# Two heads side by side in TensorE's columns: values stationary, probabilities moving

## The chip, the cores and the metric

The kernel runs on one core of one Trainium2 chip. The metric is the device time of one execution in microseconds (us). The median of three runs of the kernel before is 3547.29 us (3547.2 to 3551.07).

## The reference

A two-layer encoder over 512 tokens of width 1024. Each layer has a mixing part with 8 retention heads and 8 dilated attention heads of width 64, a cross-attention to 256 memory rows, and a product-key expert layer. The change is in the mixing part:

```python
h = rms_norm(x, norm_mix[layer])
rq, rk, rv, rg, aq, ak, av = jnp.split(h @ w_in[layer], split_points, axis=-1)
ret = bidirectional_retention(rq, rk * HEAD_DIM ** -0.5, rv, log_gamma)       # 8 heads
ret_out = head_rms_norm(ret, ret_norm_gain[layer]) * jax.nn.silu(rg)
att = dilated_mixture_attention(aq, ak, av)                                   # 8 heads
att_out = head_rms_norm(att, att_norm_gain[layer])
x = x + jnp.concatenate([ret_out, att_out], axis=-1) @ w_out[layer]
```

With all 512 tokens in one block, retention of a head is (Q K^T, times a decay that depends on the distance of the two positions) V. The three dilated patterns of attention together are one softmax over 512 keys with an additive bias per head (the slope's distance term, and the logarithm of how many patterns see the key), times V. All values are float32.

## The kernel before

Tokens stand in 4 blocks of 128 (NB = 4). `mix` runs for each layer in these steps:

- The input is normed and transposed (`norm_rows`, `to_T`) into T_hi and T_lo, a split into two parts. Projections (`proj_T` at L174, `proj_N` at L190) multiply both parts with both parts of the weights, which SP's queue loads (`wload`) and ScalarE and VectorE split (`split`, L113 and L114).
- `heads` projects queries and keys for four heads at a time (u = 0, 1) and yields, head by head, q and two key operands.
- Retention: for each head VectorE and ScalarE make the decay tile dm (L338 to L340, two buffers). For each of 4 key blocks, s = K Q^T of all 512 queries (L345; s has two PSUM buffers), and VectorE multiplies s with a window of dm into pt (L348; five buffers). Then, for each query block and key block, a matmul with 128 columns of pt stationary and the head's 64 columns of values moving adds into po, a tile of 128 queries x 4 blocks x 64 (L353). ScalarE copies po to the head's columns of cat (L355).
- `N_out` (L190, with its copy at L325) then projects the gates and the attention's values, and `norm_heads` norms four heads at once.
- Attention: for each head the bias is loaded into a dm buffer (L370). For each query block: s = Q K^T (L375), bias and row maximum on VectorE (L379, L380), exp with the row's sum on ScalarE (L381), four transposes of p into PSUM tile t (L384, two buffers), a copy to pt (L387 on ScalarE or L389 on VectorE, by the query block), and four matmuls with pt stationary and 64 columns of values moving into po (L391). At the head's end VectorE divides po by the sums into cat (L393, L394). Before head 7 (KH = 7) the memory rows are normed (`mem_norm`). Every fourth head `norm_heads` runs.
- At the end the tiles of the early pool are released, the memory's keys are projected (`mem_kv`, L174), cat is transposed (L408) and multiplied with w_out (L190).

The po tiles alternate between PSUM banks named o and g. The order in which each engine gets its instructions is not the program's alone: a scheduler orders them with a timeline of its own (`TCK`), so that projections of later heads stand between the steps of a head. Behind `mix` follow the cross-attention and routing (`tail`) and the dense and sparse expert sums (L675, L715, L578 to L590), which the change leaves alone.

Of the kernel before, what the change touches and what calls it, by code (L numbers as in the profile page):

```python
# [8 lines left out]
F32 = mybir.dt.float32  # L9
# [6 lines left out]
AF = mybir.ActivationFunctionType  # L16
OP = mybir.AluOpType
# [5 lines left out]
S = 512  # L23
L = 2
NB = 4
# [5 lines left out]
HD = 64  # L31
EPS = 1e-6
WREL = 896
# [24 lines left out]
KH = 7  # L58
# [4 lines left out]
class Kernel:  # L63
# [225 lines left out]
    def norm_heads(self, sb, cat, gain, g, silu=None):  # L289
# [12 lines left out]
            nc.vector.tensor_mul(sq, sq, silu[:, :, c])  # L302
        nc.vector.tensor_mul(v, sq, gain[:, None, c].to_broadcast([128, NB, 256]))

    def mix(self, l, kvp):
        nc, a, ps = self.nc, self.a, self.ps
        with ExitStack() as st:
            early = ExitStack()
            ea = self.pool(early, "early")
            sb = self.pool(st, "late", side="right")  # L310
            gain = sb.tile([128, D], F32, name="gain")
            self.bcast_rows(gain, a["norm_mix"], l * D, D)
            hT = (sb.tile([128, KT, S], F32R, name="T_hi"), sb.tile([128, KT, S], F32R, name="T_lo"))
            if l == 0:
                self.load_x(1, 2, 3)
            for b, h in self.norm_rows(sb, self.x, gain, order=FIRST[l]):
                self.to_T(h, hT, b * 128)
            w = a["w_in"][l]

            def N_out(c0, silu=False, order=range(NB)):  # L320
                t = ea.tile([128, NB, 512], F32, name="rv", bufs=2)

                def evac(i, c, p):
                    o = t[:, i, c:c + 256]
                    nc.scalar.activation(o, p, AF.Silu if silu else AF.Copy)  # L325
                self.proj_N(w, c0, 512, hT, order, evac)
                return t

            rv = N_out(1024, order=FIRST[l])
            lg = self.log_gamma(sb, l)  # L330
            relp = ea.tile([128, WREL], F16, name="relp")
            nc.sync.dma_start(relp, a["relpos"])
            reln = ea.tile([128, WREL], F16, name="reln")
            nc.sync.dma_start(reln, a["relneg"])
            cat = sb.tile([128, NB, D], F32, name="cat")
            for h, q, ks in self.heads(ea, w, 0, 512, hT, 1.0, HD ** -0.5):
                dm = ea.tile([128, WREL], F32, name="dm", bufs=2)
                nc.vector.tensor_scalar(dm, relp, lg[:, h:h + 1], None, op0=OP.mult)  # L338
                nc.vector.scalar_tensor_tensor(dm, reln, lg[:, 8 + h:9 + h], dm, op0=OP.mult, op1=OP.add)
                nc.scalar.activation(dm, dm, AF.Exp)  # L340
                pts = []
                for kb in range(NB):
                    s = ps.tile([128, 512], F32, name="s", bufs=2)
                    for i in range(2):
                        nc.tensor.matmul(s, ks[i][:, kb * 128:(kb + 1) * 128], q, start=(i == 0), stop=(i == 1))  # L345
                    pt = ea.tile([128, 512], F32, name="pt", bufs=5)
                    o = 384 - 128 * kb
                    nc.vector.tensor_mul(pt, s, dm[:, o:o + 512])  # L348
                    pts.append(pt)
                po = ps.tile([128, NB, HD], F32, name="og"[h % 2])  # L350
                for qb in range(NB):
                    for kb in range(NB):
                        nc.tensor.matmul(po[:, qb, :], pts[kb][:, qb * 128:(qb + 1) * 128],  # L353
                                         rv[:, kb, h * HD:(h + 1) * HD], start=(kb == 0), stop=(kb == NB - 1))
                nc.scalar.activation(cat[:, :, h * HD:(h + 1) * HD], po, AF.Copy)  # L355

            gcat = sb.tile([128, D], F32, name="gain")
            self.bcast_rows(gcat[:, :512], a["ret_norm_gain"], l * 512, 512)
            self.bcast_rows(gcat[:, 512:], a["att_norm_gain"], l * 512, 512)
            silu = N_out(1536, True)  # L360
            for g in range(2):
                self.norm_heads(sb, cat, gcat, g, silu)
            av = N_out(3072)
            den = sb.tile([128, 8, NB], F32, name="den")
            rden = sb.tile([128, 8, NB], F32, name="rden")
            for h, q, ks in self.heads(ea, w, 2048, 2560, hT, HD ** -0.5, 1.0):
                if h == KH:
                    kT = self.mem_norm(l, sb)
                bias = ea.tile([128, WREL], F32, name="dm", bufs=2)
                nc.sync.dma_start(bias, a["att_bias"][h])  # L370
                po = ps.tile([128, NB, HD], F32, name="og"[h % 2])
                for qb in range(NB):
                    s = ps.tile([128, 512], F32, name="s", bufs=2)
                    for i in range(2):
                        nc.tensor.matmul(s, q[:, qb * 128:(qb + 1) * 128], ks[i], start=(i == 0), stop=(i == 1))  # L375
                    p = ea.tile([128, 512], F32, name="p", bufs=3)
                    m = ea.tile([128, 2], F32, name="m", bufs=4)
                    o = 384 - 128 * qb
                    nc.vector.tensor_tensor_reduce(p, s, bias[:, o:o + 512], 1.0, -3e38, OP.add, OP.max, m[:, 0:1])  # L379
                    nc.vector.tensor_scalar(m[:, 1:2], m[:, 0:1], -1.0, None, op0=OP.mult)  # L380
                    nc.scalar.activation(p, p, AF.Exp, bias=m[:, 1:2], accum_out=den[:, h, qb:qb + 1])  # L381
                    tp = ps.tile([128, 4, 128], F32, name="t", bufs=2)
                    for kb in range(NB):
                        nc.tensor.transpose(tp[:, kb, :], p[:, kb * 128:(kb + 1) * 128], self.ident)  # L384
                    pt = ea.tile([128, 4, 128], F32, name="pt", bufs=5)
                    if qb % 2:
                        nc.scalar.activation(pt, tp, AF.Copy)  # L387
                    else:
                        nc.vector.tensor_copy(pt, tp)  # L389
                    for kb in range(NB):  # L390
                        nc.tensor.matmul(po[:, qb, :], pt[:, kb, :], av[:, kb, h * HD:(h + 1) * HD],  # L391
                                         start=(kb == 0), stop=(kb == NB - 1))
                nc.vector.reciprocal(rden[:, h, :], den[:, h, :])  # L393
                nc.vector.tensor_mul(cat[:, :, 512 + h * HD:512 + (h + 1) * HD], po,  # L394
                                     rden[:, h, :, None].to_broadcast([128, NB, HD]))
                if h % 4 == 3:
                    self.norm_heads(sb, cat, gcat, 2 + h // 4)

            early.close()
            kv = self.mem_kv(l, self.pool(kvp, "kv"), kT)  # L400
            next(kv)
            cst = ExitStack()
            cp = self.pool(cst, "ct")
            cT = (cp.tile([128, KT, S], F32R, name="C_hi"), cp.tile([128, KT, S], F32R, name="C_lo"))
            for k in range(KT):
                pt = ps.tile([128, NB, 128], F32, name="t", bufs=2)
                for b in range(NB):
                    nc.tensor.transpose(pt[:, b, :], cat[:, b, k * 128:(k + 1) * 128], self.ident)  # L408
                self.split(cT[0][:, k, :], cT[1][:, k, :], pt.rearrange("p b t -> p (b t)"))
# [529 lines left out]
```

## Time and profile before

| | |
|---|---|
| median of 3 runs | 3547.29 us |
| profiled execution: its time, its span | 3550.38 us, 3548.6 us |
| TensorE matmuls busy (PE) | 3473.6 us, 98% |
| weight loads busy (PEld) | 3182.7 us, 90% |
| VectorE (DVE), ScalarE (ACT), GpSimd (POOL) | 75%, 41%, 20% |
| mean granted TensorE clock | 0.991 |

PE is TensorE's matmuls and PEld its weight loads, which overlap them; a matmul's record includes its way through the array, so records overlap as well, and a busy PE is not PE at its peak. The busy time of a record says less than the distance between the starts of two. A row of a group reads: line, engine, operation, written tile <- read tiles, shapes, count | busy time in us, mean ns of one | idle time before them and what ended it. A row of the order of time or of the chain reads: start in us, length in us, what, count. TensorE's operands are named moving first: `o<-rv,pt` has rv moving and pt stationary. A matmul of two full float32 operands shows as two records.

### The profile page before, as it was taken

How to read it: one execution, taken by the hardware profiler on the slowest of the kernel's cores; microseconds unless marked ns; L12 is line 12 of the kernel's file. 1: busy time of each engine (PE TensorE's matmuls, PEld its weight loads, DVE VectorE, ACT ScalarE, POOL GpSimd, SP SyncE). 2: the span in 40 equal slices, each digit the busy share in tenths (PEclk: the TensorE clock that was granted, in tenths of full speed). 3: DMA queues.
4: the chain of work that ended last, by engine and by line, in shares of the span. 5: the costliest groups of instructions: out<-in, count | busy, mean ns of one | idle time of the engine just before them, and what ended most of it. 6: DMA issues, size and time to landing. Idle time of an engine off the chain costs nothing.

```text
span 3548.6 us, 55359 instructions
## 1 busy us (share of the span) xinstructions
PE 3473.6 (98%) x20844; PEld 3182.7 (90%) x20844; DVE 2645.4 (75%) x5722; ACT 1470.2 (41%) x2210; POOL 699.7 (20%) x518
## 2 busy tenths in 40 slices
PE   8999999999999999999999999999999999999998
PEld 7989998999888888888889899989999888888887
DVE  5565559998677788888555655599995877888885
ACT  4453544455333333333333535445553333333332
POOL 0000000002334445444100000000022443444440
PEclk9999999999999999999999999999999999999999
DMA  5252444567989999999432424446689999999992
GB/s 163 74 144 84 146 136 138 207 224 285 389 302 350 341 340 332 340 340 337 154 98 79 133 90 155 133 135 218 220 300 378 328 337 343 344 332 341 343 335 94
DMA packets 428380, 848.42 MB, mean 239 GB/s; under 512 B 28112, under 2 KB 278992, under 8 KB 421968
## 3 DMA queue, kind: packets, MB, share of 16 engines
q1 hardware_dynamic: 321360, 488.32, 41.2%
q0 software_dynamic: 73728, 268.47, 20.8%
q10 hardware_dynamic: 33024, 88.10, 6.9%
q8 instruction: 163, 2.67, 0.3%
q14 instruction: 105, 0.86, 0.1%
HBM read 754.60 MB, written 77.59 MB: 235 GB/s over the span
## 4 chain that ended last, share of the span: by engine, by line
PE 90%; DVE 6%; DMA 2%; ACT 1%; issue 1%; SPq 0%; ACTq 0%; POOL 0%; DVEq 0%; POOLq 0%
PE pj L675 28%; PE pj L174 13%; PE s L715 10%; PE t L715 10%; PE pj L190 9%; PE o L715 5%; PE g L715 5%; PE s L345 1%; DVE w_lo L114 1%; PE g L391 1%; PE s L375 1%; PE t L384 1%; PE g L353 1%; PE o L353 1%; PE g L873 1%
## 5 line engine op out<-in xcount | busy, mean ns | idle before, releaser
L114 DVE TENSOR_TENSOR w_lo<-w_raw,w_hi 128x1024 fp32r<-128x1024 f32 x696 | 849.4, 1222 | 404.1 <-ACT w_hi L113 391.7
L113 ACT ACTIVATE w_hi<-w_raw 128x1024 fp32r<-128x1024 f32 x696 | 735.3, 1060 | 981.6 <-PE g L715 342.8
L578 POOL DMA_INDIRECT row<-in_expert_down,ei x256 | 339.0, 1324 | 2308.3 <-PE g L874 916.8
L675 PE MATMUL pj<-hT_hi,w_hi 128*128 128x384 f32 x2048 | 697.7, 341 | 12.8 <-ACT c L678 10.5
L675 PE MATMUL pj<-hT_lo,w_hi 128*128 128x384 f32 x2048 | 698.8, 341 | 0.0
L675 PE MATMUL pj<-hT_hi,w_lo 128*128 128x384 f32 x2048 | 696.0, 340 | 0.8 <-DVE w_lo L114 0.6
L578 POOL DMA_INDIRECT row<-in_expert_up,ei x256 | 360.0, 1406 | 454.2 <-DVE x L590 419.3
L675 PEld LDWEIGHTS pj<-hT_hi,w_hi 128*128 128x128 f32 x2048 | 386.3, 189 | 18.3 <-ACT c L678 11.1
L675 PEld LDWEIGHTS pj<-hT_hi,w_lo 128*128 128x128 f32 x2048 | 386.1, 189 | 5.6 <-DVE w_lo L114 2.4
L675 PEld LDWEIGHTS pj<-hT_lo,w_hi 128*128 128x128 f32 x2048 | 386.2, 189 | 4.4
L590 DVE SCALAR_TENSOR_TENSOR x<-row,act,x 128x1024 f32<-128x1024 f32 x256 | 327.7, 1280 | 6.0 <-DMA row<-in_expert_up,ei 4.6
L584 DVE SCALAR_TENSOR_TENSOR row<-row,hn 128x1024 f32<-128x1024 f32 x256 | 309.4, 1219 | 19.9 <-DMA row<-in_expert_down,ei 19.5
L113 ACT ACTIVATE ch<-c 128x384 fp32r<-128x384 f32 x128 | 67.0, 523 | 280.2 <-PE g L715 240.1
L715 PE MATMUL t<-w_lo,ch 128*128 128x512 f32 x512 | 160.7, 389 | 0.0
L715 PE MATMUL t<-w_hi,ch 128*128 128x512 f32 x512 | 159.6, 389 | 0.0
L715 PE MATMUL s<-w_hi,ch 128*128 128x512 f32 x512 | 158.5, 391 | 0.0
L715 PE MATMUL s<-w_lo,ch 128*128 128x512 f32 x512 | 158.1, 390 | 0.0
L190 PE MATMUL pj<-w_hi,T_hi 128*128 128x256 f32 x640 | 156.9, 286 | 0.9 <-ACT T_hi L113 0.5
L715 PE MATMUL s<-w_hi,cl 128*128 128x512 f32 x512 | 157.8, 389 | 0.0
L715 PE MATMUL t<-w_hi,cl 128*128 128x512 f32 x512 | 157.7, 389 | 0.0
L113 ACT ACTIVATE ch<-cd 128x384 fp32r<-128x384 f32 x128 | 66.6, 520 | 208.9 <-PE g L715 208.9
L174 PE MATMUL pj<-T_hi,w_hi 128*128 128x512 f32 (+1 forms) x512 | 150.0, 341 | 2.1 <-DVE qlo L260 1.8
(260 smaller groups left out, 7291.9 us busy)
## 6 DMA issues: line engine op xcount, KB each, us to landing
w_raw<-in_down_T SPq DMA_DIRECT2D x256, 512.0 KB
w_raw<-in_expert_up SPq DMA_DIRECT2D x256, 512.0 KB
Gd<-mq ACTq DMA_DIRECT2D x48, 1024.0 KB
gt<-Gd SPq DMA_DIRECT2D x32, 1536.0 KB
w_raw<-in_peer_w_query SPq DMA_DIRECT2D x64, 512.0 KB
w_raw<-in_w_in SPq DMA_DIRECT2D x56, 512.0 KB
Cd<-c ACTq DMA_DIRECT2D x128, 192.0 KB
cd<-Cd SPq DMA_DIRECT2D x128, 192.0 KB
```

The costliest lines, as they stand in the source:

```text
L113: self.nc.scalar.activation(hi, src, AF.Copy)
L114: self.nc.vector.tensor_sub(lo, src, hi)
L174: nc.tensor.matmul(ps[:, :T], wt[k // 4][x][:, k % 4, s * 128:(s + 1) * 128], hT[y][:, k, :T], start=(k == 0 and x == y), stop=(k == KT - ...
L190: nc.tensor.matmul(ps[:, :256], hT[x][:, k, ts], wt[k // 4][y][:, k % 4, :], start=(k == 0 and x == y), stop=(k == KT - 1 and (x, y) == pa ...
L345: nc.tensor.matmul(s, ks[i][:, kb * 128:(kb + 1) * 128], q, start=(i == 0), stop=(i == 1))
L353: nc.tensor.matmul(po[:, qb, :], pts[kb][:, qb * 128:(qb + 1) * 128], rv[:, kb, h * HD:(h + 1) * HD], start=(kb == 0), stop=(kb == NB - 1))
L375: nc.tensor.matmul(s, q[:, qb * 128:(qb + 1) * 128], ks[i], start=(i == 0), stop=(i == 1))
L578: nc.gpsimd.indirect_dma_start(out=t, out_offset=None, in_=tab, in_offset=bass.IndirectOffsetOnAxis(ap=ei[:, j:j + 1], axis=0))
L584: nc.vector.scalar_tensor_tensor(t, t, 1.0, self.hn, op0=OP.mult, op1=OP.mult, accum_out=act[:, j:j + 1])
L590: nc.vector.scalar_tensor_tensor(x, t, act[:, j:j + 1], x, op0=OP.mult, op1=OP.add)
L675: k.nc.tensor.matmul(pa[:, :ND], x[:, kk, :], y[:, kk, :], start=(kk == 0 and x is dh and y is hi), stop=(kk == KT - 1 and x is dl))
L715: self.k.nc.tensor.matmul(self.acc[b, h], cc[x][:, s], uu[y][:, h * 512:(h + 1) * 512], start=(b, h) not in self.started, stop=last and x ...
```

## The change

Heads are taken two at a time. For a pair, the matmul of probabilities and values has the head's 64 columns of values stationary and the probabilities moving; the even head writes output partitions 0 to 63 and the odd head 64 to 127 of one tile po, which thus holds the outputs with head columns on partitions and queries along the free dimension. In retention a matmul moves all 512 queries of pt for one key block, and the products follow after every two key blocks of both heads. In attention one moves the 128 queries of a block, the heads alternating. When a pair is complete, `turned` copies po to SBUF (oT) and transposes it in four pieces into PSUM tile t, from which cat is written for both heads at once. Both heads' decay or bias tiles are made or loaded before the pair's first score. In attention the copy to pt is on ScalarE for the odd head and on VectorE for the even one, and the memory rows are normed before the last pair.

```diff
+    def half_av(self, po, h, v, pt, kb):
+        r = slice(64 * (h % 2), 64 * (h % 2) + 64)
+        self.nc.tensor.matmul(po[r, :], v[:, h * HD:(h + 1) * HD], pt, start=(kb == 0), stop=(kb == NB - 1))
+
+    def turned(self, sb, po):
+        t = sb.tile([128, S], F32, name="oT")
+        self.nc.scalar.activation(t, po, AF.Copy)
+        tp = self.ps.tile([128, NB, 128], F32, name="t", bufs=2)
+        for qb in range(NB):
+            self.nc.tensor.transpose(tp[:, qb, :], t[:, qb * 128:(qb + 1) * 128], self.ident)
+        return tp
...
-            for h, q, ks in self.heads(ea, w, 0, 512, hT, 1.0, HD ** -0.5):
-                dm = ea.tile([128, WREL], F32, name="dm", bufs=2)
...
-                po = ps.tile([128, NB, HD], F32, name="og"[h % 2])
-                for qb in range(NB):
-                    for kb in range(NB):
-                        nc.tensor.matmul(po[:, qb, :], pts[kb][:, qb * 128:(qb + 1) * 128],
-                                         rv[:, kb, h * HD:(h + 1) * HD], start=(kb == 0), stop=(kb == NB - 1))
-                nc.scalar.activation(cat[:, :, h * HD:(h + 1) * HD], po, AF.Copy)
+            it = self.heads(ea, w, 0, 512, hT, 1.0, HD ** -0.5)
+            for m, two in enumerate(zip(it, it)):
+                dms = []
+                for h, q, ks in two:
+                    dm = ea.tile([128, WREL], F32, name="dm", bufs=2)
...
+                po = ps.tile([128, 512], F32, name="og"[m % 2])
+                for k0 in range(0, NB, 2):
+                    pts = []
+                    for kb in range(k0, k0 + 2):
+                        for (h, q, ks), dm in zip(two, dms):
+                            s = ps.tile([128, 512], F32, name="s", bufs=2)
...
+                            nc.vector.tensor_mul(pt, s, dm[:, o:o + 512])
+                            pts.append((kb, h, pt))
+                    for kb, h, pt in pts:
+                        self.half_av(po, h, rv[:, kb], pt, kb)
+                tp = self.turned(ea, po)
+                nc.scalar.activation(cat[:, :, m * 128:(m + 1) * 128], tp, AF.Copy)
...
-            for h, q, ks in self.heads(ea, w, 2048, 2560, hT, HD ** -0.5, 1.0):
-                if h == KH:
+            it = self.heads(ea, w, 2048, 2560, hT, HD ** -0.5, 1.0)
+            for m, two in enumerate(zip(it, it)):
+                if m == 3:
                     kT = self.mem_norm(l, sb)
-                bias = ea.tile([128, WREL], F32, name="dm", bufs=2)
-                nc.sync.dma_start(bias, a["att_bias"][h])
+                biases = []
+                for h, q, ks in two:
+                    bias = ea.tile([128, WREL], F32, name="dm", bufs=2)
+                    nc.sync.dma_start(bias, a["att_bias"][h])
+                    biases.append(bias)
+                po = ps.tile([128, 512], F32, name="og"[m % 2])
                 for qb in range(NB):
...
-                    if qb % 2:
-                        nc.scalar.activation(pt, tp, AF.Copy)
-                    else:
-                        nc.vector.tensor_copy(pt, tp)
                     for kb in range(NB):
-                        nc.tensor.matmul(po[:, qb, :], pt[:, kb, :], av[:, kb, h * HD:(h + 1) * HD],
-                                         start=(kb == 0), stop=(kb == NB - 1))
-                nc.vector.reciprocal(rden[:, h, :], den[:, h, :])
-                nc.vector.tensor_mul(cat[:, :, 512 + h * HD:512 + (h + 1) * HD], po,
-                                     rden[:, h, :, None].to_broadcast([128, NB, HD]))
+                        for h, pt in pts:
+                            self.half_av(po[:, qb * 128:(qb + 1) * 128], h, av[:, kb], pt[:, kb, :], kb)
+                tp = self.turned(ea, po)
...
+                nc.vector.tensor_mul(cat[:, :, c].rearrange("p b (h d) -> p b h d", d=HD),
+                                     tp.rearrange("p b (h d) -> p b h d", d=HD),
+                                     rden[:, hs, :].rearrange("p h b -> p b h")[:, :, :, None].to_broadcast([128, NB, 2, HD]))
```

More of the change, by code (lines that the diff above doesn't have):

```diff
@@ L335, in mix @@
             cat = sb.tile([128, NB, D], F32, name="cat")
-            for h, q, ks in self.heads(ea, w, 0, 512, hT, 1.0, HD ** -0.5):
-                dm = ea.tile([128, WREL], F32, name="dm", bufs=2)
[L338 to L341, printed above, removed]
-                for kb in range(NB):
[L343 to L349, printed above, removed]
-                po = ps.tile([128, NB, HD], F32, name="og"[h % 2])
-                for qb in range(NB):
-                    for kb in range(NB):
-                        nc.tensor.matmul(po[:, qb, :], pts[kb][:, qb * 128:(qb + 1) * 128],
-                                         rv[:, kb, h * HD:(h + 1) * HD], start=(kb == 0), stop=(kb == NB - 1))
-                nc.scalar.activation(cat[:, :, h * HD:(h + 1) * HD], po, AF.Copy)
@@ new lines, in mix @@
+            it = self.heads(ea, w, 0, 512, hT, 1.0, HD ** -0.5)
[3 more added lines that the diff above has]
+                    dm = ea.tile([128, WREL], F32, name="dm", bufs=2)
+                    nc.vector.tensor_scalar(dm, relp, lg[:, h:h + 1], None, op0=OP.mult)
+                    nc.vector.scalar_tensor_tensor(dm, reln, lg[:, 8 + h:9 + h], dm, op0=OP.mult, op1=OP.add)
+                    nc.scalar.activation(dm, dm, AF.Exp)
+                    dms.append(dm)
+                po = ps.tile([128, 512], F32, name="og"[m % 2])
[4 more added lines that the diff above has]
+                            s = ps.tile([128, 512], F32, name="s", bufs=2)
+                            for i in range(2):
+                                nc.tensor.matmul(s, ks[i][:, kb * 128:(kb + 1) * 128], q, start=(i == 0), stop=(i == 1))
+                            pt = ea.tile([128, 512], F32, name="pt", bufs=5)
+                            o = 384 - 128 * kb
+                            nc.vector.tensor_mul(pt, s, dm[:, o:o + 512])
[4 more added lines that the diff above has]
+                nc.scalar.activation(cat[:, :, m * 128:(m + 1) * 128], tp, AF.Copy)
@@ new lines, in mix @@
+                biases = []
[4 more added lines that the diff above has]
+                po = ps.tile([128, 512], F32, name="og"[m % 2])
+                for qb in range(NB):
+                    pts = []
+                    for (h, q, ks), bias in zip(two, biases):
+                        s = ps.tile([128, 512], F32, name="s", bufs=2)
+                        for i in range(2):
+                            nc.tensor.matmul(s, q[:, qb * 128:(qb + 1) * 128], ks[i], start=(i == 0), stop=(i == 1))
+                        p = ea.tile([128, 512], F32, name="p", bufs=3)
+                        mx = ea.tile([128, 2], F32, name="m", bufs=4)
+                        o = 384 - 128 * qb
+                        nc.vector.tensor_tensor_reduce(p, s, bias[:, o:o + 512], 1.0, -3e38, OP.add, OP.max, mx[:, 0:1])
+                        nc.vector.tensor_scalar(mx[:, 1:2], mx[:, 0:1], -1.0, None, op0=OP.mult)
+                        nc.scalar.activation(p, p, AF.Exp, bias=mx[:, 1:2], accum_out=den[:, h, qb:qb + 1])
+                        tp = ps.tile([128, 4, 128], F32, name="t", bufs=2)
+                        for kb in range(NB):
+                            nc.tensor.transpose(tp[:, kb, :], p[:, kb * 128:(kb + 1) * 128], self.ident)
+                        pt = ea.tile([128, 4, 128], F32, name="pt", bufs=5)
+                        if h % 2:
+                            nc.scalar.activation(pt, tp, AF.Copy)
+                        else:
+                            nc.vector.tensor_copy(pt, tp)
+                        pts.append((h, pt))
+                    for kb in range(NB):
+                        for h, pt in pts:
+                            self.half_av(po[:, qb * 128:(qb + 1) * 128], h, av[:, kb], pt[:, kb, :], kb)
@@ new lines, in mix @@
+                tp = self.turned(ea, po)
+                hs = slice(2 * m, 2 * m + 2)
+                nc.vector.reciprocal(rden[:, hs, :], den[:, hs, :])
+                c = slice(512 + m * 128, 512 + (m + 1) * 128)
+                nc.vector.tensor_mul(cat[:, :, c].rearrange("p b (h d) -> p b h d", d=HD),
+                                     tp.rearrange("p b (h d) -> p b h d", d=HD),
+                                     rden[:, hs, :].rearrange("p h b -> p b h")[:, :, :, None].to_broadcast([128, NB, 2, HD]))
@@ L399, in mix @@
+                if m % 2:
+                    self.norm_heads(sb, cat, gcat, 2 + m // 2)
             early.close()
```

16 lines of the change are left out of this document (removed).

## The prediction

> **What bounds the kernel now.** I read the page first (busy time, then the chain that ended last), because a change to matmuls is worth nothing where TensorE isn't the limit.
>
> ```profile
> span 3548.6 us, 55359 instructions
> PE 3473.6 (98%) x20844; PEld 3182.7 (90%) x20844; DVE 2645.4 (75%) x5722; ACT 1470.2 (41%) x2210; POOL 699.7 (20%) x518
> PE 90%; DVE 6%; DMA 2%; ACT 1%; issue 1%; SPq 0%; ACTq 0%; POOL 0%; DVEq 0%; POOLq 0%
> ```
>
> TensorE is busy 98% of the span and carries 90% of the chain. Time taken off it in one stage therefore comes off the end, unless another engine ends last in that stage. The stages here are `mix` of layer 0 (up to about 300 us) and of layer 1. So I next read busy times by stretch, for the spare time of each engine there (columns: length, PE, PEld, DVE, ACT, POOL, clock, DMA share, GB/s).
>
> ```profile
> 160.00:180.00 20.00, 20.00 (x156) 19.27 (x155) 11.44 (x20) 6.57 (x11) 0.00 (x0) 1.00 0.24 76
> 220.00:240.00 20.00, 20.00 (x124) 17.57 (x123) 12.06 (x31) 10.71 (x22) 0.00 (x0) 1.00 0.50 133
> 240.00:260.00 20.00, 18.37 (x132) 16.77 (x131) 13.73 (x40) 13.28 (x31) 0.00 (x0) 0.91 0.65 181
> 260.00:280.00 20.00, 18.88 (x148) 16.95 (x147) 19.19 (x76) 11.69 (x28) 0.00 (x0) 1.00 0.08 25
> 280.00:300.00 20.00, 19.63 (x168) 18.95 (x167) 11.69 (x25) 10.41 (x17) 0.00 (x0) 1.00 0.18 54
> ```
>
> TensorE is full until 240 us. At the end of attention it idles 1 to 2 us in 20, its clock falls to 0.91 once, and VectorE is at 19.19 of 20 between 260 and 280 us: there a faster TensorE will in part only wait.
>
> **What is removed.** The products of probabilities and values (L353 for retention, L391 for attention) have pt stationary, 128 columns, and 64 columns of values moving. Rows by line and shape:
>
> ```profile
> L353 PE MATMUL g<-rv,pt 128*128 128x64 f32 x256 | 32.0, 268 | 0.0
> L353 PE MATMUL o<-rv,pt 128*128 128x64 f32 x256 | 32.0, 268 | 0.0
> L391 PE MATMUL g<-rv,pt 128*128 128x64 f32 x256 | 32.3, 272 | 0.0
> L391 PE MATMUL o<-rv,pt 128*128 128x64 f32 x256 | 31.8, 270 | 0.0
> ```
>
> The code issues 8 heads x 16 matmuls x 2 layers = 256 of each kind, and the rows count 512 of each: a full f32 matmul is two records. The mean of 268 ns is not its price, since records overlap; the price is the distance between starts. The chain in order of time gives it:
>
> ```profile
> 77.17 2.85 PE o L353 x26
> 217.44 1.73 PE o L391 x16
> 258.50 0.84 PE o L391 x8
> 219.17 0.88 PE t L384 x8
> 256.29 0.47 PE s L375 x2
> 292.82 7.27 PE pj L174 x60
> ```
>
> 2.85 / 26 = 0.110 us and 1.73 / 16 = 0.108 us a record. Removed: 512 x 0.110 + 512 x 0.108 = 56.3 + 55.3 = **111.6 us**, all on the path wherever TensorE is full.
>
> **What is added on TensorE.** The values (64 columns) are stationary, pt moves, and the even head writes output partitions 0 to 63, the odd one 64 to 127. What a moving column costs in f32 I read from memory attention, the f32 matmul with 256 moving columns (order of time):
>
> ```profile
> 423.50 1.89 PE L502 MATMUL o<-a,mv 128*128 128x256 f32 x8
> L502 PE MATMUL o<-a,mv x128: 377/379/634, 414.2 to 2284.6; 128*128 128x256 f32 x128
> ```
>
> (1.89 - 0.38) / 7 = 0.216 us per record of 256 columns; so 0.431 for 512 (estimate, doubled) and 0.108 for 128 (halved). Retention has 64 matmuls of 512 columns: 128 records x 0.431 = 55.2 us one after the other. Attention has 256 of 128 columns: 512 x 0.108 = 55.3 us. One after the other, then, the swap gains 111.6 - 110.5 = 1.1 us: the empty half of the array has replaced the costly weight load. The gain hangs on whether two heads' records run side by side. No row here has an instruction on half of the array, so I bound it: nothing overlaps (110.5 us), or two at a time. Two records of one matmul use the same half and can't overlap each other. With records started in order, a1 a2 b1 b2, a2 waits for a1, and b1 runs beside a2: n alternating matmuls take n + 1 slots, not 2n.
>
> How many stand together depends on the order. The retention stretch of before shows that the products into one output tile keep the order of the program:
>
> ```profile
> 71.22 0.33 PE L353 MATMUL o<-rv,pt 128*128 128x64 f32 x2
> 71.91 0.33 PE L353 MATMUL o<-rv,pt 128*128 128x64 f32 x2
> 76.55 0.33 PE L353 MATMUL o<-rv,pt 128*128 128x64 f32 x2
> 77.00 3.01 PE L353 MATMUL o<-rv,pt 128*128 128x64 f32 x26
> ```
>
> With the first pt all four query blocks could have begun; only one matmul (2 records) goes, then the next with the second pt, and 26 records when the last pt is there. Both heads now write one tile, so they will alternate as written. In retention the pts arrive in twos (s has two buffers), so I take groups of two: 3 of 4 slots, 55.2 x 3/4 = **41.4 us** (whole pairs together, 9 of 16: 31.0). In attention I take the first product alone, because the odd head's pt comes later, and the other seven together: 2 + 8 = 10 of 16 slots, 34.6 us (9 of 16: 31.1).
>
> The Trainium skill (TensorE: Matmul & The Clock Gate, Part 3) says that matmuls in different column groups run at the same time and gives 2.38x for three tiles; no run here shows it yet, and by that ratio the sum would lie between my two ends.
>
> `turned` adds 4 transposes for each of 16 pairs: 64 x 0.88/8 = **7.0 us** of TensorE.
>
> **Changing between whole array and halves.** Before never does it. The nearest changes, from s to o at 71.22 us, follow at the normal distance, which would make it free. The other end is that the array runs empty: a record's length less its slot.
>
> ```profile
> 76.09 0.40 PE L174 MATMUL pj<-T_hi,w_hi 128*128 128x512 f32 x1
> 76.32 0.39 PE L174 MATMUL pj<-T_lo,w_hi 128*128 128x512 f32 x1
> ```
>
> 0.39 - 0.23 = 0.16 us. Retention: 4 groups in each of 8 pairs, two changes each, 64; attention: 2 groups for each of 4 query blocks, 128. 192 changes cost 0 to 31 us. The free end comes from changes that leave the array whole, so I don't trust it fully and take a third: **10 us**.
>
> **What lies beside TensorE.**
>
> ```profile
> L355 ACT ACTIVATE cat<-g x8: 385/386/387, 93.3 to 1927.5; 128x256 f32<-128x256 f32 x8
> L387 ACT ACTIVATE pt<-t 128x512 f32<-128x512 f32 x32 | 19.0, 594 | 28.6 <-PE t L384 28.4
> L348 DVE TENSOR_TENSOR pt<-s,dm 128x512 f32<-128x512 f32 x64 | 43.0, 688 | 45.8 <-PE s L345 45.5
> L394 DVE TENSOR_TENSOR cat<-g,rden 128x256 f32<-128x256 f32 x4 | 1.7, 419 | 0.8 <-PE g L391 0.8
> SPq L370 <- DMA dm<-in_att_bias: 3.0, 1, 3.0
> ```
>
> Retention: two copies of 0.386 become two of 0.594 (oT and cat), 0.42 us more ScalarE for each pair; attention: one copy of 0.594 more. VectorE does one 512-wide multiply (as the 0.69 us one of L348, estimated) for two of 0.419. ScalarE is at 7 to 13 of 20 us: no cost. Behind the last retention pair TensorE has projections (160 to 180 us, full), so the added latency there is covered too. At the end of attention the turn adds a copy and four transposes, 0.59 + 0.44 = 1.0 us, before the norm of the last heads; the memory projection (L174 x60 at 292.82) covers it. Without that cover it costs 1 us in each layer.
>
> The two dm buffers now hold one pair's biases. A pair's first bias is loaded when the even head's last score is used, not a whole head ahead. Its load waits on SP for that read, and weight loads queued behind it wait too; they run four buffers ahead. A bias takes 3.0 us to land by the row of SP's waits; two scores of 1.75 us each (t, s and o at about 0.44 + 0.47 + 0.84) pass meanwhile. Two such changes of pair in each layer lie past the projections: 0 to 12 us, I take **3**. For VectorE's full stretch, where L391's records stand:
>
> ```profile
> 250.00:293.00 43.00, 19.16 (x152) 19.18 (x152) 0.98 0.14 42
> ```
>
> 152 of the layer's 256, so 0.6 of attention's saving of 20.7 us: 0 to 12 us can be lost to VectorE, I take a third, **4**.
>
> **The sum:** -111.6 + 41.4 + 34.6 + 7.0 + 10 + 3 + 4 = -11.6 us. The profiled execution took 3550.4 us (span 3548.6), 3.1 above the median of 3547.3. 3550.4 - 11.6 = 3538.8 there, and 3535.7 against the median: **3536**. About 0.2% (7 us) is what this kernel's measurement can tell from no change. With the overlap as assumed and changes between 0.01 and 0.09 us each, the likeliest case's own range is 3527 to 3543.
>
> **The rivals.**
>
> *Full overlap.* Whole pairs alternate and changes are free: -111.6 + 31.0 + 31.1 + 7.0 + 7 = -35.5, so 3512. For: strict order in a tile, which gives long alternating groups. Against: pts come one at a time, 0.69 us apart.
>
> *Halves don't run together* (the hardware runs f32 records singly, or other matmuls stand between the two heads): the change then doesn't do what it says. 110.5 + 7.0 - 111.6 = +5.9, with 10 for changes and 3 for biases +19: 3566; with free changes and no bias wait 3553. For: no row shows two matmuls at once, and s is computed between pts. Against: the outputs are disjoint.
>
> *The array runs empty at each change.* Place: each border of a group of halves; price 0.16 us x 192 = 31: -28.6 + 31 + 7 = +9, 3557, slower. It decides from (28.6 - 7) / 192 = 0.11 us for each change; between about 0.07 and 0.14 nothing can be measured. For: a half's weights may not load while the whole array works. Against: s to o costs nothing.
>
> The Trainium skill (TensorEngine Tiling (Array Packing), Key Properties) states that changing the tiling mode drains TensorE; by that sentence this rival's sign would hold, and no run here shows it.
>
> **How the numbers follow.** Forecast 0.42 (0.03 of it within 0.2%); full overlap 0.13; empty array at 0.07 to 0.14 us, no change, 0.12; above that, slower, 0.08; singly 0.25, of which 0.06 within 0.2%. Faster: 0.39 + 0.13 = 0.52; same: 0.03 + 0.12 + 0.06 = 0.21; slower: 0.08 + 0.19 = 0.27. The range reaches to the full overlap (3512, less 3 for its bias term: 3509) and to singly with its wait terms (3566).
>
> **What would show it.** Side by side: in the chain or the order of time, records of the two heads start in twos, with a mean distance near 0.32 us (retention) and 0.07 to 0.08 us (attention) within a group, against 0.43 and 0.11 if singly. A price of changes: a gap above 0.23 us between a whole-array record and the first half record, or behind the last. Biases and VectorE: idle TensorE time before s or t past the last projection, released by p of L379's kind, and a clock below 1. The prediction is wrong if the heads' products stand apart in TensorE's order, or if the end of attention keeps its length although the products shrink.

## The result, and the profile after

The changed kernel takes 3585.21 us (median of 4 runs, 3584.3 to 3586.48) against 3547.39 us (3547.2 to 3551.07): 1.0104 times as long [1.0091, 1.0116], 37.8 us slower. The forecast was 3536, with a range from 3509 to 3566. The profiled execution of the kernel after took 3585.85 us.

From the page of the kernel after, the lines that answer to the first three of before:

```profile
span 3584.1 us, 54723 instructions
PE 3490.7 (97%) x20524; PEld 3116.1 (87%) x20524; DVE 2647.7 (74%) x5706; ACT 1480.5 (41%) x2218; POOL 679.8 (19%) x518
PE 89%; DVE 5%; DMA 3%; ACT 1%; issue 1%; SPq 0%; ACTq 0%; DVEq 0%; POOLq 0%
```

TensorE has 320 records fewer, and is busy 17 us longer in a span 35.5 us longer. Where that lies is read from three rows of the groups by line in each kernel: first and last start of the retention scores, of the attention scores, and of the memory-attention scores behind `mix`. Of these I use the first start only (the first number behind the three durations). Before, then after:

```profile
L345 PE MATMUL s<-Q,K x64: 387/397/478, 64.7 to 151.1; 128*128 128x512 f32 x64
L375 PE MATMUL s<-K,Q x64: 387/397/775, 199.3 to 276.5; 128*128 128x512 f32 x64
L479 PE MATMUL s<-mk,mq x32: 377/379/382, 390.8 to 413.9; 128*128 128x256 f32 x32
```

```profile
L367 PE MATMUL s<-Q,K x64: 387/397/504, 65.2 to 159.9; 128*128 128x512 f32 x64
L401 PE MATMUL s<-K,Q x64: 387/397/796, 206.1 to 300.7; 128*128 128x512 f32 x64
L510 PE MATMUL s<-mk,mq x32: 377/379/382, 409.1 to 432.2; 128*128 128x256 f32 x32
```

From these come two lengths for each layer, used for every kernel below. R, from the first retention score to the first attention score, goes from 134.6 to 140.9 us (layer 1 the same). A, from there to the first memory score, goes from 191.5 to 203.0 (layer 1: 189.3 to 203.0). Over both layers that is +12.6 and +25.2 = +37.8 us: the whole loss lies in these two stages (the rest of the two profiled executions differs by 2.3 us the other way, which leaves the 35.5 of the spans). The part from layer 0's memory scores to layer 1's retention, which the change leaves alone, takes 1443.1 and 1441.3 us; over all executions below it varies from 1438 to 1452, so for differences of a few us the stages say more than the whole time.

**The halves do run side by side.** TensorE's order of time in the kernel after, first around retention products, then around attention products; the second row of the first fence is the same group, asked for over 10 ns only:

```profile
76.39 0.63 PE L367 MATMUL s<-Q,K 128*128 128x512 f32 x2
76.95 0.65 PE L309 MATMUL o<-pt,rv 128*64 128x512 f32 x2
76.95 1.08 PE L309 MATMUL o<-pt,rv 128*64 128x512 f32 x4
77.96 0.73 PE L367 MATMUL s<-Q,K 128*128 128x512 f32 x2
78.53 0.39 PE L174 MATMUL pj<-T_lo,w_hi 128*128 128x512 f32 x1
...
82.25 0.39 PE L174 MATMUL pj<-T_hi,w_lo 128*128 128x512 f32 x1
82.58 1.07 PE L309 MATMUL o<-pt,rv 128*64 128x512 f32 x2
83.58 0.73 PE L367 MATMUL s<-Q,K 128*128 128x512 f32 x2
```

```profile
223.23 0.40 PE L174 MATMUL pj<-T_hi,w_hi 128*128 128x512 f32 x1
223.55 1.09 PE L309 MATMUL o<-pt,rv 128*64 128x128 f32 x14
224.57 0.66 PE L410 MATMUL t<-ident,p 128*128 128x128 f32 x4
225.16 0.43 PE L309 MATMUL o<-pt,rv 128*64 128x128 f32 x2
```

A group of 4 records, two of each head, lasts 1.08 us; a group of 2 records of one head 1.07. Inside the first, the two heads' records start 6 ns apart (76.951 and 76.957), and both lie in the 0.65 us of the second row. The 14 records of attention, 8 of one head and 6 of the other, take 8 slots.

**But every group of half records pays at both its borders.** Compare the distances between starts with those of before. Into the half: the second score starts at 76.39 + 0.23 = 76.62, the first half record at 76.95, 0.33 later instead of 0.23. The group takes 77.96 - 76.95 = 1.01 (83.58 - 82.58 = 1.00 with two records), against 0.86 for two slots of 0.431. The next two whole-array records take 78.53 - 77.96 = 0.57 instead of the 0.47 of two scores, and are 0.73 long instead of 0.63. Sum: 0.10 + 0.14 + 0.10 = 0.34 us for a group of half records, with two records or with four.

**And in retention most groups are half empty.** In TensorE's order 54 groups hold the 64 retention products: 44 of one matmul, 10 of two. In attention there are 60: 28 of one matmul, 28 of seven, 4 of eight. So 114 x 0.34 = 38.8 us go to borders. That is a little high: behind 42 of attention's 60 groups stands a transpose, and the record after it starts 0.165 us later instead of 0.109, so these cost 0.30 and all groups together 37.1. I keep the one figure, 0.34, below.

**The rest is waiting at the end of attention.** Busy time from the first attention score to the first memory score of layer 0, and over 165 us that hold the end of attention in layer 1, before and after (columns: length, PE, PEld, DVE, ACT, POOL, clock, DMA share, GB/s):

```profile
199.30:390.80 191.50, 188.21 (x1440) 178.21 (x1439) 115.57 (x271) 93.76 (x166) 0.00 (x0) 0.99 0.41 121
1985.00:2150.00 165.00, 162.22 (x1292) 155.25 (x1292) 100.30 (x240) 78.86 (x142) 0.00 (x0) 1.00 0.38 117
```

```profile
206.10:409.10 203.00, 191.77 (x1456) 168.36 (x1455) 115.14 (x263) 96.61 (x170) 0.00 (x0) 0.98 0.38 114
1985.00:2150.00 165.00, 153.31 (x1109) 128.56 (x1108) 92.84 (x223) 77.37 (x142) 0.00 (x0) 0.98 0.34 101
```

TensorE idles 3.3 us before and 11.2 us after (2.8 and 11.7 in layer 1), by length less PE. TensorE's waits in the two stretches of layer 0 (us in total, times, longest):

```profile
PE t L384 <- ACT p L381: 1.9, 2, 1.6
PE t L123 <- DVE T_hi L114: 0.9, 1, 0.9
```

```profile
PE t L123 <- DVE T_lo L462: 2.9, 1, 2.9
PE g L309 <- ACT pt L413: 2.7, 3, 2.0
PE t L317 <- ACT oT L314: 1.6, 3, 0.7
PE t L123 <- DVE cat L424: 1.3, 1, 1.3
PE s L401 <- DVE m L405: 1.2, 3, 0.5
PE t L410 <- DVE cat L424: 0.7, 2, 0.4
```

These are five kinds of wait that before does not have: for the norm of the memory rows (L462), for the odd head's copy of p (L413), for the copy and the multiply that turning needs (L314, L424), and for the scores' buffer, which the row maximum frees (L405).

The second of these has a cause that is not new. Around its longest case ScalarE and then TensorE do this (the number in brackets is the idle time before):

```profile
249.36 1.06 ACT L460 ACTIVATE T_lo<-T_lo 128x1024 f32<-128x1024 f32 x1 [2.25 <-DMA T_lo<-in_mem]
250.53 0.60 ACT L413 ACTIVATE pt<-t 128x512 f32<-128x512 f32 x1
251.18 1.98 PE L309 MATMUL g<-pt,rv 128*64 128x128 f32 x16 [2.01 <-ACT pt L413]
```

ScalarE stands waiting for the load of the memory rows, whose squares it is to take for their norm; the copy of p, whose transposes had ended by 248.3, comes behind that, and TensorE waits for the copy. In the kernel before ScalarE waits 1.96 us for the same load, and the 1.6 us that TensorE waits for p (L381) come right behind it.

### The profile page after: what moved, and what is told of

It reads as the page before. It is cut to its first block, busy times and chain, and to the rows that moved or that the text cites. A ratio compares the mean times of both kernels' runs of the same rounds, so it can differ in the third digit from the quotient of the medians.

```text
span 3584.1 us, 54723 instructions
## 1 busy us (share of the span) xinstructions
PE 3490.7 (97%) x20524; PEld 3116.1 (87%) x20524; DVE 2647.7 (74%) x5706; ACT 1480.5 (41%) x2218; POOL 679.8 (19%) x518
## 4 chain that ended last, share of the span: by engine, by line
PE 89%; DVE 5%; DMA 3%; ACT 1%; issue 1%; SPq 0%; ACTq 0%; DVEq 0%; POOLq 0%
PE pj L706 28%; PE pj L174 13%; PE pj L190 10%; PE s L746 10%; PE t L746 10%; PE o L746 5%; PE g L746 5%; PE g L309 1%; PE o L309 1%; PE s L367 1%; DVE w_lo L114 1%; PE t L410 1%; PE o L533 1%; PE s L510 1%; PE g L904 1%
## 5 line engine op out<-in xcount | busy, mean ns | idle before, releaser
L609 POOL DMA_INDIRECT row<-in_expert_up,ei x256 | 344.9, 1347 | 472.4 <-DVE x L621 435.7
```

Of the source, the lines that this page charges most:

```text
L609: nc.gpsimd.indirect_dma_start(out=t, out_offset=None, in_=tab, in_offset=bass.IndirectOffsetOnAxis(ap=ei[:, j:j + 1], axis=0))
```

## The experiments

Each ratio, and each difference behind a ratio, is to the kernel before, measured again with the experiment (medians from 3550.2 to 3551.1 us). "The change" is the kernel after. Its 3585.2 us stand against 3547.4, so a difference between its median and that of an experiment can be 3 us off; R and A are the surer measure.

**One half of the change at a time.** `e1_retention_only` has the pairs in retention and the old loop in attention; `e2_attention_only` the other way round.

```diff
 e1, attention:
-            it = self.heads(ea, w, 2048, 2560, hT, HD ** -0.5, 1.0)
-            for m, two in enumerate(zip(it, it)):
+            for h, q, ks in self.heads(ea, w, 2048, 2560, hT, HD ** -0.5, 1.0):
...
 e2, retention:
-            it = self.heads(ea, w, 0, 512, hT, 1.0, HD ** -0.5)
-            for m, two in enumerate(zip(it, it)):
+            for h, q, ks in self.heads(ea, w, 0, 512, hT, 1.0, HD ** -0.5):
...
```

> Pairs of heads in halves for retention alone; attention as in the kernel before. Theory 1 (borders: the halves do run together, but every group of half-array records costs about 0.34 us for going to halves and back, and retention's products stand in 54 groups): 54 groups at 1.00 us and 0.2 us around them instead of 56.3 us, and 3.5 us of transposes, so +12 to +15 us on the kernel before. Theory 2 (the loss is nearly all waiting at the end of attention, for biases and for the memory rows): 0 to +4 us, since projections cover retention's waits. Theory 3 (halves run singly): 55.2 + 3.5 - 56.3 = +2.4 us without borders.

> Pairs of heads in halves for attention alone; retention as in the kernel before. Theory 1 (borders): 60 groups, 48.6 us and 60 x 0.2 us around them against 55.3 us, and 3.5 us of transposes: +9 us, and not more than that by borders alone. Theory 2 (waits at the end of attention): the changed kernel's TensorE idles 17 us more in the two attention stretches; with that +20 to +27 us. The two single changes should add up to the whole change's +38 us within 5 us if neither works through the other.

Retention alone: 3560.97 us, 1.0033 [1.002, 1.0045], +10.8; R 140.9 in both layers, A as before (191.6, 190.7). Attention alone: 3579.57 us, 1.0087 [1.007, 1.0103], +29; R 134.6, A 203.9 and 204.0. The two add up to 40 of 38: each part loses by itself, in its own stage, and nothing arises from both.

**Longer groups.** `e3_last_first` starts each group with the head and key block whose pt comes last, so that no half record can start before its partner is ready:

```diff
-                    for kb, h, pt in pts:
-                        self.half_av(po, h, rv[:, kb], pt, kb)
+                    for kb, h, pt in reversed(pts):
+                        self.half_av(po, h, rv[:, kb], pt, kb == 1, kb == 2)
...
-                        for h, pt in pts:
+                        for h, pt in reversed(pts):
```

(half_av takes its start and stop from the last two arguments; retention's key blocks then run 1, 0, 3, 2.)

> The whole change, with the products of a group begun by the pt that is ready last (odd head and last key block first), so that none can start alone and a group stands together: 16 groups of 8 records in retention, 32 groups of 16 in attention, instead of 54 and 60. Theory 1 (borders): 66 groups fewer at 0.34 us, 22 us, and in retention 44 records no longer alone; retention 16 x (1.73 + 0.34) = 33 us instead of 66, attention 32 x (0.86 + 0.34) = 39 us instead of 61: 25 to 55 us less than the changed kernel, 3530 to 3560 us. Theory 2 (waits): within 8 us of the changed kernel's 3585 us. Theory 3 (halves run singly): the 0.34 us are not saved where the records still take 0.43 and 0.108 us each, at most 22 us less, 3563 us or more.

3558.1 us, 1.0024 [1.0012, 1.0035]: 27 us less than the change by the medians, 30 by what each loses against before. Order of time:

```profile
81.32 1.94 PE L309 MATMUL o<-pt,rv 128*64 128x512 f32 x8
...
223.55 1.09 PE L309 MATMUL o<-pt,rv 128*64 128x128 f32 x16
```

16 groups of 8 records and 32 of 16 in place of 114: the next record follows the first row at 83.18, 1.86 us later, which is 4 slots of 0.431 and 0.14. R falls to 127.3 and 127.2, 13.6 less than after and 7.3 less than before: in retention longer groups turn the loss into a gain. By the terms above, 38 groups fewer x 0.34 = 12.9 and 44 slots fewer (108 to 64) x 0.431 = 19.0 would give 31.9 in two layers; 27.3 came. Most of what is missing is new idle time: TensorE stands still for 3.1 us of R in each layer, against 1.1 in the change. In attention the groups are as long as they can be, and yet A is 202.0 and 200.7. Its loss is not the borders alone.

**The same groups, one head after the other.** `e4_head_by_head` differs from e3 only in the order inside a group: all matmuls of the odd head, then all of the even one.

```diff
-                    for kb, h, pt in reversed(pts):
+                    for kb, h, pt in sorted(pts, key=lambda x: (-x[1], -x[0])):
...
-                    for kb in range(NB):
-                        for h, pt in reversed(pts):
+                    for h, pt in reversed(pts):
+                        for kb in range(NB):
```

> The same groups as with the last pt first, but within a group all records of the odd head and then all of the even one, so only one half works at a time; nothing else differs. Theory 1 (halves run together when records alternate): the groups take twice as long, retention 16 x 1.73 = 28 us more, attention 32 x 0.86 = 28 us more: 40 to 56 us slower than with alternation, part of it hidden at the end of attention. Theory 3 (halves run singly anyway): the same time as with alternation within 5 us. If the queue reorders records far enough to pair the heads by itself, the time lies between.

3568.26 us, 1.0052 [1.0036, 1.0069]: 10 us more than e3: neither the 40 to 56 of theory 1 nor the 5 of theory 3, but the case in between that was named.

```profile
81.31 1.94 PE L309 MATMUL o<-pt,rv 128*64 128x512 f32 x8
...
224.56 1.58 PE L309 MATMUL o<-pt,rv 128*64 128x128 f32 x16
```

The 8 retention records, 4 of one head followed by 4 of the other, take no longer than alternating ones. The 16 in attention take 12 slots, where one after the other is 16 and alternating 8: four records alone (224.563, .723, .832, .941), then eight in twos (225.050 and 225.056, then 225.159 and 225.216, and so on), then four alone; all 32 groups do so. The ninth record of the program started with the fifth. Two readings fit, and no run decides between them: TensorE takes a record whose half is free ahead of some three that stand before it, or the scheduler, which orders the instructions, had already put the even head's first matmul ahead of the odd head's last. The profile does not hold the order in which TensorE was given them. Either way the order in the program mattered less than I thought, and what stands between two heads matters more.

**The waits of attention.** `e5_three_bias` is e3 with a third bias buffer (oT takes a pt buffer instead of one of its own, for room):

```diff
-                    bias = ea.tile([128, WREL], F32, name="dm", bufs=2)
+                    bias = ea.tile([128, WREL], F32, name="dm", bufs=3)
...
-        t = sb.tile([128, S], F32, name="oT")
+        t = sb.tile([128, S], F32, name="pt", bufs=5)
```

(the same for retention's dm.) `e6_mem_late` is e3 with the memory rows' norm issued late, in the middle of the last pair, ahead of its third query block:

```diff
-                if m == 3:
-                    kT = self.mem_norm(l, sb)
...
                 for qb in range(NB):
+                    if m == 3 and qb == 2:
+                        kT = self.mem_norm(l, sb)
```

`e7_both_waits` has both edits, and `e9_change_mem_late` the late norm alone, on the change; their edits are those shown.

> Last pt first, and three dm buffers instead of two (oT takes a pt buffer to make room), so that the next pair's first bias can be loaded a whole pair ahead. Theory 2a (the wait for the bias between pairs): the bias waits of about 1 to 4 us for each change of pair go, 5 to 12 us less than with last pt first alone. Theory 2b (the wait comes from the memory rows' norm, which now stands a head earlier and blocks ScalarE's queue): within 3 us of it.

> Last pt first, and the memory rows' norm issued in the middle of the last pair (before its third query block) instead of ahead of it. Theory 2b: ScalarE no longer waits there for the memory's load, TensorE's gap of 2 to 3.4 us ahead of the products near the fifth of attention goes, and so do the two gaps at the memory's transposes: 5 to 15 us less than with last pt first alone. Theory 2a: within 3 us, or slower by up to 5 us because the memory's keys are then late as a cover for the end.

> Last pt first with both: three dm buffers and the late norm of the memory rows. If both theories hold their part, the two gains add up: 10 to 25 us less than with last pt first alone, 3535 to 3548 us. If the end of attention is bound by the pace of VectorE and ScalarE instead, less than the sum of the two single gains.

> The whole change as it was made, with only the memory rows' norm moved to the middle of the last pair. If that norm, a head earlier in the change, costs what it cost with last pt first (15 us, both layers), 3568 to 3573 us. If it cost so much only because TensorE had been made faster there, 0 to 8 us less than the changed kernel, 3577 to 3585 us.

A third bias buffer: 3559.55 us, 1.0026 [1.0016, 1.0035], no different from e3 in the whole time. A is 200.5 and 197.8, 1.5 and 2.9 less than in e3; attention left as it was varies by as much (189.3 to 191.7 in before, e1, e8 and e10), so a small gain is neither shown nor ruled out. The late norm: 3543.84 us, 0.998 [0.997, 0.9989], 14 us less than e3, and A falls by 6.2 us in each layer, to 195.8 and 194.5. Both: 3541.61 us, 0.9975 [0.9965, 0.9986], no clear step further. In e3 TensorE waited before the memory rows' transposes (the number in brackets is the idle time before):

```profile
269.93 0.66 PE L123 MATMUL t<-ident,T_lo 128*128 128x128 f32 x4 [1.39 <-DVE cat L424]
...
273.48 1.94 PE L123 MATMUL t<-ident,T_lo 128*128 128x128 f32 x8 [2.89 <-DVE T_lo L462]
```

With the late norm that wait is 0.19:

```profile
276.15 0.66 PE L123 MATMUL t<-ident,T_lo 128*128 128x128 f32 x4 [0.19 <-DVE T_hi L114]
```

The diff moved `mem_norm` from head 7 to the last pair, which is head 6: its transposes stand in TensorE's queue ahead of the last heads' products and hold them up until VectorE has normed. The edit does not move ScalarE's share of the norm: the first square stands at 235.08 us in e3 and at 233.80 in e6, and in both TensorE waits behind it (3.4 and 2.0 us). On the change itself the same edit gives less: 3580.56 us, 1.0088 [1.0071, 1.0104], 5 us less by the medians, with A 198.5 in both layers (-4.5 each); of the two cases named, 15 or 0 to 8, the second. About half of the 4.5 is idle time (9.4 us in A, after 11.2 and 11.7); the rest goes with the granted clock, 1.00 in both layers instead of 0.98, at which TensorE is busy 189.1 us instead of 191.8 and 191.3. Why the clock rose is not shown.

**Retention alone, in long groups.** `e8_retention_last_first` is e3 in retention and the old loop in attention, put back as in e1.

> Last pt first in retention, attention as in the kernel before. Retention's 16 groups take 31.5 us and 16 x 0.2 us around them instead of 56.3, with 3.5 us of transposes: 18 us less than the kernel before if TensorE alone counts there. Attention's start came 7.1 us earlier in a layer with last pt first, so 14 us less, 3532 to 3538 us. If the time saved in retention is taken back by waits later in the layer: 0 to 5 us less.

3542.61 us, 0.9978 [0.9968, 0.9988]. R 127.2 and 127.3, 14.7 us less in two layers than before; the whole gains 8 by the medians, between the two cases named (14, or 0 to 5). The profiled execution took 5.5 us more than the median, and in it the untouched middle is 5 us longer than in before; what the median execution lost of the 14.7 is not on record.

**Without halves.** `e10_whole_array` is e1 with the same order of work, but all 128 columns of a pair's values stationary for each head; each head writes its own PSUM bank, half of it unused, and two copies of 64 partitions take the halves that count.

```diff
-        self.nc.tensor.matmul(po[r, :], v[:, h * HD:(h + 1) * HD], pt, start=(kb == 0), stop=(kb == NB - 1))
+        c = h // 2 * 128
+        self.nc.tensor.matmul(po[h % 2], v[:, c:c + 128], pt, start=(kb == 0), stop=(kb == NB - 1))
```

> Pairs in retention alone as in the first experiment, but the stationary operand is the pair's 128 value columns for both heads, so every product uses the whole array: pt moves through it as before, each head writes a bank of its own, the half of it that belongs to the other head is not used, and two copies of 64 partitions fill oT. No half is ever used, and nothing can run side by side. Theory 1 (borders cost about 0.34 us a group): 128 records x 0.431 = 55.2 us without borders instead of 66 us: 8 to 13 us less than halves in retention alone, within 5 us of the kernel before. If instead a record of 512 moving columns costs more than 0.431 us, or the loss lies in the transposes and copies: the same time as halves in retention alone, or slower.

3556.08 us, 1.0019 [1.0009, 1.0028]. The whole time is 4.9 us less than e1's, where 8 to 13 were expected, but R is 135.2 and 135.3, 5.6 us less than e1 in each layer, though no two heads share a slot. Its chain in order of time:

```profile
71.15 0.86 PE o L309 x2
...
76.20 0.86 PE g L309 x2
```

Two records are 0.86 us, 0.43 each, with no border around them (1.00 in e1). From this the border comes a second time: e1 loses 11.3 us in two layers although 10 of its groups hold two heads that share slots (10 x 0.86 = 8.6), so 19.9 / 54 = 0.37 us a group, against 0.34 from the starts. (The middle was 12 us longer in this execution than in e1's, which hides part of it in the whole time.)

**Fewer heads in halves.** `e11_first_half` is e3 in retention and in heads 0 to 3 of attention; heads 4 to 7 and the norm of the memory rows are as before. The forecast was that attention's first heads, under the projections, would gain.

```diff
-            for m, two in enumerate(zip(it, it)):
+            for m in range(2):
+                two = next(it), next(it)
...
+            for h, q, ks in it:
...
```

> Last pt first in retention and in attention's heads 0 to 3, where projections still fill TensorE; heads 4 to 7, at the end of attention, and the norm of the memory rows as in the kernel before. Theory (the halves pay where TensorE is full, and their longer chain costs where it is not): on retention's 14 us in the stage, attention's first two pairs save 4 x 1.73 - 4 x 1.22 - 0.44 = 1.6 us a pair, 6 us in both layers, and no new gap of TensorE opens at the end: 3530 to 3537 us, 13 to 20 us less than the kernel before. Rival (attention in halves costs by its borders and transposes wherever it stands): 3541 us or more, no better than last pt first in retention alone.

3541.8 us, 0.9974 [0.9965, 0.9984]; R 127.3, A 196.6 and 193.3, against 191.7 and 191.4 with attention left alone. The gain did not come. In layer 0 the memory rows' load falls into that stage:

```profile
235.44 1.06 ACT L491 ACTIVATE T_lo<-T_lo 128x1024 f32<-128x1024 f32 x1 [4.51 <-DMA T_lo<-in_mem]
237.26 1.98 PE L309 MATMUL g<-pt,rv 128*64 128x128 f32 x16 [4.27 <-ACT pt L412]
```

TensorE waits 4.27 us there in one piece, against 1.8 at the same place in e8, and its granted clock over the first 50.4 us of A is 0.93, against 0.98 in e8. These two, 2.5 us more of the wait and an estimated 0.05 x 45 = 2.3 for the clock, are as large as the 4.9 by which layer 0 is longer than in e8. In layer 1 A is 1.9 longer; there TensorE idles 7.8 us, against 3.3 in e8, in several waits of at most 1.4. So the forecast's condition, that no new gap opens, did not hold; and its rival, that halves cost by their borders wherever they stand, is not shown by this run either. e6, e7, e8 and e11 are all 0.2 to 0.3% faster than before and can't be told apart.

**What stays open** is why attention in long groups does not gain. For e6, one layer: removed 27.7; 16 groups x 8 slots x 0.108 = 13.8, 16 x 0.34 = 5.4 and transposes 1.75 come in, so -6.7, but A is 4.3 us longer than before, 11.0 off. Idle TensorE accounts for 7 of these:

```profile
192.40:388.20 195.80, 185.72 (x1455) 164.85 (x1454) 114.73 (x263) 96.33 (x170) 0.00 (x0) 0.98 0.39 118
```

```profile
PE t L410 <- DVE cat L424: 2.1, 3, 1.4
PE g L309 <- ACT pt L413: 2.0, 1, 2.0
PE t L317 <- ACT oT L314: 1.8, 3, 0.7
PE s L401 <- DVE m L405: 1.7, 4, 0.9
PE t L410 <- ACT p L407: 1.0, 2, 0.7
```

10.1 us idle against 3.3. The second row is the memory rows' load again, as long as before's. The others name the chain score, maximum, exp, transposes, copy, product, turn, multiply, with both heads of a pair needed before TensorE may go on; no run took one of these away by itself, and the remaining 4 are not accounted for.

## Why the prediction was wrong

The sum was -11.6 us; +37.8 came. The step that failed most is the price of changing between the whole array and halves, a third of what an emptied array would cost, taken from a row in which the array stays whole; next come the waits at the end of attention. Term by term, by its own steps:

- **Halves side by side: right.** Rows of two heads start 6 ns apart and take the time of one. The rival "halves don't run together" is false of the array. The Trainium skill (TensorE: Matmul & The Clock Gate, Part 3) draws tiles starting about 4 ns apart, near the 6 of these rows; it also has matmuls start strictly in program order, and whether e4's ninth record, which started with the fifth, breaks that is open, since the order given to TensorE is not on record.
- **Attention's slots: right.** 34.6 predicted; 28 groups of 2 slots and 32 of 8, 312 slots at 0.108 to 0.109, are 33.9. The first product did go alone. The rule behind it, n + 1 slots for n matmuls, was not right: two matmuls of two heads take two slots, not three (1.01 us as a group, like 1.00 for one), and eight take eight. Seven take eight either way, so the agreement is partly luck.
- **Retention's groups: failed.** I took groups of two matmuls, as the pts arrive; 44 of 54 groups hold one, since scores and projections stand between. 54 x 0.862 = 46.5 instead of 41.4: the rival's second reason ("other matmuls stand between the two heads") was right here, and the fix was an order, as e3 shows.
- **Borders: the term that broke it.** Predicted 10 us: 96 groups with 192 changes, at a third of 0.16. Measured 114 groups x 0.34 = 38.8, or 0.17 for a change, about the end that I had called an empty array (0.16). The row I trusted, s to o at the normal distance, leaves the array whole, and says nothing of a change that doesn't; e10, whole array throughout, shows the same freedom. Of the rivals the empty array had the right place, sign and size: it was to decide from 0.11. That the array empties is read from that size alone; e10 shows that the price comes with the halves. I gave the slower part of that rival 0.08. The Trainium skill (TensorEngine Tiling (Array Packing), Key Properties) says that a change of mode drains TensorE; the trace agrees as far as a price of 0.34 us for the way in and out goes, and I gave that rule too little weight.
- **Transposes of the turn: 7.0** as predicted, by their count.
- **Waits: 7 predicted, 16.8 measured, and some 5 for the clock.** These terms make -111.6 + 46.5 + 33.9 + 38.8 + 7.0 = +14.6. In retention that closes: -56.3 + 46.5 + 54 x 0.34 + 3.5 = +12.1 against 12.6. In attention it leaves 25.2 - 2.5 = 22.7. Idle TensorE makes 16.8 of it; the clock, 0.98 for 0.99 in layer 0 and 0.98 for 1.00 in layer 1, about 5 more (an estimate, 0.01 x 203 + 0.02 x 165). With 0.30 for the groups ahead of transposes 2 us more stay open. The bias buffers that I priced at 3 cost nothing that e5 shows beyond the scatter of A. What I did not price was in the diff: `mem_norm` one head earlier (12 us in two layers when e6 moves it, 9 when e9 does, half of it with the clock), and the copy, turn and multiply of each pair, for which I had named a cover: the waits for oT and cat are 1.6 + 1.3 + 0.7 us in layer 0 of after.
- **What would show it:** the gaps "above 0.23 us between a whole-array record and the first half record, or behind the last" were named, and are there (0.33); so were idle time before s or t and a clock below 1. The twos are there too, where the heads stand together.

## What to carry to other kernels

Before splitting the array, count the groups, not the matmuls: each group of half-array records cost 0.30 to 0.34 us here, so a group must save more than that (four slots of 512 columns, two heads each, saved 1.7 us against one head after the other; one lone matmul saved nothing and paid in full). Let a group start with the operand that is ready last, so that an order which issues whatever can go does not break it up. And treat every call that a diff carries along to another place as a change of its own, with the queue behind it.

## What the runs showed of the hardware

- Going from whole-array to half-array float32 records and back cost 0.10 us on entering, 0.14 in the group and 0.10 in the records behind it (0.06 where these are transposes), alike for groups of 2, 4 and 8 records (1.00, 1.01 and 1.86 us for 2, 2 and 4 slots of 0.431).
- Two half-array float32 records of different halves start 6 ns apart and take the time of one (1.01 us for two of each half, 1.00 for two of one half).
- A load can hold up an engine that does not use it: ScalarE stood 2.25 us for the memory rows' load, the copy of p came only behind their square, and TensorE idled 2.01 us for that copy (the kernel after; 4.51 and 4.27 in e11).
- A half-empty array costs nothing by itself: 64 stationary columns and 128 took the same 0.43 us a record of 512 columns (e1 less its border, e10).
